# Up projection of a ConvFFN: seven of 22 pairs of channel tiles by seven half products, with sums of weights formed in DRAM

## The chip, the cores and the metric

One core of one Trainium2 chip. Its engines each run an instruction queue of their own: TensorE (PE) multiplies, VectorE (DVE) and ScalarE (ACT) work elementwise, GpSimd (POOL) does a little of both and issues the DMAs that add into their target, SyncE (SP) issues the other DMAs. The metric is the device time of one execution in microseconds (us).

## What is computed

The kernel is one layer of an encoder block, for 512 tokens of 1024 channels in fp32: a layer norm, then a mixing stage (a scan branch and a sparse attention branch, joined and projected by `w_out`), a layer norm, a feed-forward stage with a causal convolution over time, and a last layer norm. The change is in the feed-forward stage, of which the reference says:

```python
def _conv_ffn(h, w_up, conv_w, conv_b, w_down):
    u = _causal_dwconv(h @ w_up, conv_w, conv_b)
    a, v = jnp.split(u, 2, axis=-1)
    return (jax.nn.silu(a) * v) @ w_down

h = _layernorm(DN_ALPHA * h + mix, ln1_g, ln1_b)
f = _conv_ffn(h, ffn_w_up, ffn_conv_w, ffn_conv_b, ffn_w_down)
```

`w_up` is 1024×5632: 2816 channels for a and as many for v. The convolution has three taps.

## The kernel before

**Products.** Each fp32 operand is split into a high and a low half (ACT copies the high one, DVE subtracts for the low one), and a product is three matmuls, hi·hi, lo·hi and hi·lo (`mm3`, whose matmuls stand under L231). A weight block of 128×1024 comes by one SP DMA into one of four `wraw` buffers, then ACT forms `whi` (L188) and DVE `wlo` (L189), in one of three pairs of `whi`/`wlo` buffers (`wload`, L178). The code asks the scheduler to place these steps early.

**w_out.** The projection before the feed-forward stage accumulates in eight PSUM banks, two for each of the four tiles of 128 tokens (L255). Token tile after token tile is finished, normalized (DVE, POOL) and transposed, four blocks of 128 at a time, into one of two `ptr` banks (L1177). ACT and DVE split the transposed block into `h1hi` and `h1lo` (L174, L175), the token operand of the up projection. The low halves of the last of w_out's other operand, `mlo`, lie in the two buffers of the tag `y8`.

**Up projection.** 44 tiles of 128 channels, two by two: tile 2n is a, tile 2n+1 is v, so that pair n gives 128 channels of the result. A tile is 8 blocks of 128 input channels times three matmuls of 512 token columns, 24 matmuls. The first three tiles run in halves of 256 tokens, 144 matmuls, so that they can begin before the last token tiles are transposed. The banks go round among the `pacc` tiles and `pa`, `pb`, `pc`.

**Behind each pair** stands `up_out`: for a and for v one ACT operation (the last tap and the bias, L1270) and two DVE operations (the other taps, L1273) read the tile from PSUM; then Silu on ACT (L1276) and the product on DVE (L1278). Every second pair goes on into `operands` (L1247 to L1253), which forms the sums of channels that the down projection uses. The down projection itself already goes by seven half products, and the sums of its weights are formed in DRAM during the up projection, by `sums_of`: one copy on SP's queue and three adding DMAs on POOL's queue for each of 11 blocks (`sd_d`, L206 to L219).

**Attention.** Earlier, in the attention branch, POOL adds mask and bias of a head and a query block into `tm` (L986), 64 times; DVE and ACT then form the softmax.

Of the kernel before, what the change touches and what calls it, by code (L numbers as in the profile page):

```python
# [9 lines left out]
F32 = mybir.dt.float32  # L10
# [6 lines left out]
P = 128  # L17
# [40 lines left out]
def tok(i):  # L58
    return slice(i * P, (i + 1) * P)
# [11 lines left out]
def block_kernel(ctx, tc, A, out):  # L71
# [16 lines left out]
    def wt(tag, shape, name, dtype=F32):  # L88
        return wk.tile(shape, dtype, name=name, tag=tag, bufs=BUFS[tag])
# [9 lines left out]
    def ct(shape, name, dtype=F32):  # L99
        return cst.tile(shape, dtype, name=name, tag=name)  # L100
# [59 lines left out]
    nc.gpsimd.memset(e_t, math.e)  # L160


    last_pow, last_w = [None], [None]

    def rsqrt_small(src, scale, eps, n, i=0):

# [6 lines left out]
    def split(hi, lo, src):  # L173
        nc.scalar.activation(hi, src, AF.Copy)  # L174
        return nc.vector.tensor_tensor(lo, src, hi.bitcast(F32), OP.subtract)  # L175

    def wload(src, ahead=400, dst=None):

        cols = src.shape[1]
        with tc.high_priority(offset=ahead):  # L180
            raw = wrw.tile([P, D], F32, name="wraw", tag="wraw")
            last_w[0] = nc.sync.dma_start(raw[:, :cols], src)
            if dst is None:
                hi = whl.tile([P, D], F32R, name="whi", tag="whi")
                lo = whl.tile([P, D], F32R, name="wlo", tag="wlo")
            else:
                hi, lo = dst
            nc.scalar.activation(hi[:, :cols], raw[:, :cols], AF.Copy)  # L188
            nc.vector.tensor_tensor(lo[:, :cols], raw[:, :cols], hi[:, :cols].bitcast(F32),  # L189
                                    OP.subtract)  # L190
        return hi, lo

    def w_halves(name, s):
# [9 lines left out]
    def w_(name, s, **kw):  # L203
        return wload(A[name][s], **kw)

    def sums_of(c):  # L206

        S_, B_ = sd_d[c], A["w_dq"][c]

        def copy():  # L210
            with tc.issue_after(last_w[0].ins):
                nc.sync.dma_start(S_, B_)

        def add(dst, src):
            with tc.issue_after(last_pow[0].ins):
                nc.gpsimd.dma_start(dst, src, accum_op=OP.add)  # L216
# [750 lines left out]
    class Head:  # L967
# [12 lines left out]
        def exp(self, i):  # L980
            Q, Kh, Kl = self.qk
            hh = self.hh
            K = P * (i + 1)
            f = max(K - 2 * P, 0)
            tm = wt("tn", [P, 2 * P], "tm")
            nc.gpsimd.tensor_tensor(tm[:, :K - f], maskt[i][:, f:], self.toe[:, 2 * P - K + f:], OP.add)  # L986
            p = tr_tile()
            mm(p[:, :K], Q[:, hh, tok(i)], Kh[:, hh, :K], start=True, stop=False)
            mm(p[:, :K], Q[:, hh, tok(i)], Kl[hh][:, :K], start=False, stop=True)
            if i > 1:  # L990
                self.L.append(wt("v", [P, T], "l"))
            l = self.L[i]
            ic = slice(i, i + 1)
            if f:
                nc.vector.tensor_tensor_reduce(l[:, :f], p[:, :f], maskt[i][:, :f], scale=1.0, scalar=3.0e38,
                                               op0=OP.add, op1=OP.min, accum_out=self.mf[:, ic])
            nc.vector.tensor_tensor_reduce(l[:, f:K], p[:, f:K], tm[:, :K - f], scale=1.0,  # L997
                                           scalar=self.mf[:, ic] if f else 3.0e38,
                                           op0=OP.add, op1=OP.min, accum_out=self.mn[:, ic])
            nc.scalar.activation(l[:, :K], l[:, :K], AF.Exp, bias=self.mn[:, ic], scale=-1.0,  # L1000
                                 accum_out=self.sm[:, ic])
# [157 lines left out]
    for i in range(NT):  # L1159
        for h in range(2):  # L1160
            for k in range(KR, KD):
                tok_mm(accs[2 * i + h], mT[k], wo[k], i, h, False, k == KD - 1)
            ws = half_of(h)
            nc.vector.scalar_tensor_tensor(h1[i][:, ws], h1[i][:, ws], ALPHA, accs[2 * i + h], OP.mult, OP.add)
        mv, rs = ln_stats(h1[i])
        for j in range(2):
            t = h1[i][:, half_of(j)]
            if j == 1 and i < NT - 1:
                nc.vector.tensor_scalar(t, t, mv[:, 0:1], rs, OP.subtract, OP.mult)
                nc.gpsimd.tensor_tensor(t, t, l1r["g", j], OP.mult)  # L1170
                nc.gpsimd.tensor_tensor(t, t, l1r["b", j], OP.add)
            else:
                nc.vector.scalar_tensor_tensor(t, t, mv[:, 0:1], l1r["g", j], OP.subtract, OP.mult)
                nc.vector.scalar_tensor_tensor(t, t, rs, l1r["b", j], OP.mult, OP.add)
            tr = v3(tr_tile())
            for k in range(4):
                nc.tensor.transpose(tr[:, k], h1[i][:, tok(4 * j + k)], ident)  # L1177
# [7 lines left out]
    NS, NC = 8, KF // 2  # L1185
    TH = T // 2
    L_, R_ = slice(0, TH), slice(TH, T)
    fp = E(tc.tile_pool(name="f", bufs=1, reuse_waits="tile"))
    cnt = {"x": 0, "f": 0}
    f8 = {}  # L1190

# [68 lines left out]
    def up_out(n, pa, pb):  # L1260
        uv = []
        key = [(2 * n + j + 1) * UP - 2 * KF * UP if n > KF - 3 else None for j in range(2)]

        def k(j, t):
            return None if key[j] is None else key[j] + t

        for j, p in enumerate((pa, pb)):
            c = n + j * KF
            y = wt("v", [P, T], "u")
            at(S, k(j, 0), nc.scalar.activation(y, p, AF.Identity, bias=fb[:, c:c + 1], scale=fw[:, 88 + c:89 + c]))  # L1270
            for i in (1, 0):
                d = 2 - i
                at(V, k(j, 1.5), nc.vector.scalar_tensor_tensor(  # L1273
                    y[:, d:], p[:, :T - d], fw[:, 44 * i + c:44 * i + c + 1], y[:, d:], OP.mult, OP.add))
            uv.append(y)
        at(S, k(0, 3), nc.scalar.activation(uv[0], uv[0], AF.Silu))  # L1276
        if n < 2 * NS:
            nc.vector.tensor_tensor(uv[0], uv[0], uv[1], OP.mult)  # L1278
            even.append(uv[0])
            if len(even) == 2:  # L1280
                operands(*even)
                even.clear()
        else:
            fO[n] = o_tile()
            tt(k(1, 2.5), fO[n], uv[0], uv[1], OP.mult)

    w = [w_("w_up", s) for s in range(3)]
    accs = [acc_tile() for _ in range(3)]
    for ts in (slice(0, 2 * P), slice(2 * P, T)):
        for j in range(3):  # L1290
            proj(accs[j][:, ts], w[j], [[x[:, ts] for x in h] for h in h1T])
    pend = accs
    done = 0
    jobs = [sums_of(c) for c in range(NC)]
    for s in range(3, 2 * KF + 1):
        if len(pend) >= 2:
            up_out(done, pend[0], pend[1])
            done += 1
            pend = pend[2:]
        if s < 2 * KF:  # L1300
            p = acc_tile() if s % 2 else any_tile("abc")
            proj(p, w_("w_up", s), h1T)
            pend.append(p)
            if s == 36:
                mark = last_w[0]
        if s % 3 == 0:
            for c, j in enumerate(jobs):
                if 0 <= s // 3 - 1 - c < 4:
                    j[s // 3 - 1 - c]()
        if s == 8:  # L1310
            for i in range(NT):
                nc.sync.dma_start(h1_d[:, i], h1[i])

# [329 lines left out]
```

## Time and profile before

| What | Value |
|---|---|
| Median of three runs | 1083.81 us (1083.75 to 1083.89) |
| The profiled execution's own time | 1083.8 us |
| Its span (first to last instruction) | 1082.1 us |
| PE busy | 1070.2 us, 99% |
| DVE busy | 829.6 us, 77% |
| ACT busy | 503.1 us, 46% |
| POOL busy | 195.1 us, 18% |
| w_out ends, up projection begins | 727.28 us |
| First full tile of the up projection begins | 746.68 us |

All positions are microseconds from the span's start. The span is 1.7 us shorter than the execution's own time. A row of a group reads: line, engine, operation, out<-in, shapes and count; busy time and mean ns of one; idle time of the engine just before them, and what ended it. Matmul ends are modelled and overlap the next start, so the time from start to start is what one costs.

### The profile page before, as it was taken

The numbers are of one execution on the slowest core, as the hardware profiler recorded it, in microseconds if no ns is written. First come the engines' busy times: TensorE is split into PE (matmuls) and PEld (weight loads), VectorE is DVE, ScalarE is ACT, GpSimd is POOL, SyncE is SP. The second block draws the span as 40 slices with busy tenths as digits, with TensorE's granted clock in tenths as the row PEclk, the third lists the DMA queues.
The fourth block names the chain that finished last, engine by engine and source line by source line (L and its number), as shares of the span: only waits on it lengthen the run. The fifth ranks groups of instructions, "written<-read, shape, count | busy, mean of one in ns | idle before, by whom it ended". The sixth has DMA issues, their size and how long they took to land.

```text
span 1082.1 us, 14878 instructions
## 1 busy us (share of the span) xinstructions
PE 1070.2 (99%) x5397; PEld 890.4 (82%) x5397; DVE 829.6 (77%) x1509; ACT 503.1 (46%) x876; POOL 195.1 (18%) x214
## 2 busy tenths in 40 slices
PE   8999999999999999999999999999999999999997
PEld 7888888888888888888778778889888888888886
DVE  7667787886999996558989958665766676559697
ACT  5444665563643642355556434313544444345631
POOL 3000203203013023013323442042111111000001
PEclk9999999999999999999999999999999999999999
DMA  7442423474344243322212454818889888226653
GB/s 286 141 146 88 134 80 119 144 217 137 96 119 137 79 141 108 124 86 74 88 56 72 141 195 154 293 59 198 195 237 228 202 237 230 96 90 231 212 181 123
DMA packets 54378, 161.64 MB, mean 149 GB/s; under 512 B 6273, under 2 KB 10929, under 8 KB 54129
## 3 DMA queue, kind: packets, MB, share of 16 engines
q1 hardware_dynamic: 49552, 149.16, 41.9%
q0 software_dynamic: 4752, 11.54, 7.3%
q8 instruction: 42, 0.69, 0.3%
q14 instruction: 32, 0.25, 0.1%
HBM read 152.12 MB, written 34.76 MB: 173 GB/s over the span
## 4 chain that ended last, share of the span: by engine, by line
PE 97%; DMA 1%; DVE 1%; ACT 0%; issue 0%; POOL 0%; DVEq 0%
PE pacc L231 65%; PE pc L231 8%; PE ptr L231 6%; PE pb L231 6%; PE pa L231 5%; PE pacc L255 2%; PE ptr L255 1%; PE pa L234 1%; PE ptr L234 1%; PE pb L234 1%; DMA htok_d<-x 1%; PE pb L255 1%; PE pc L255 1%; PE pa L255 1%; DMA x<-in_x_dram 0%; DVE x_st L339 0%
## 5 line engine op out<-in xcount | busy, mean ns | idle before, releaser
L189 DVE TENSOR_TENSOR wlo<-wraw,whi 128x1024 fp32r<-128x1024 f32 x141 | 184.4, 1308 | 124.3 <-ACT whi L188 123.1
L188 ACT ACTIVATE whi<-wraw 128x1024 fp32r<-128x1024 f32 x141 | 149.1, 1058 | 225.4 <-PE pacc L231 148.7
L231 PE MATMUL pacc<-hhi,whi 128*128 128x512 f32 (+1 forms) x536 | 216.4, 404 | 0.8 <-ACT hhi L398 0.8
L231 PE MATMUL pacc<-hlo,whi 128*128 128x512 f32 (+1 forms) x536 | 209.9, 392 | 0.5 <-DVE hlo L401 0.5
L231 PE MATMUL pacc<-hhi,wlo 128*128 128x512 f32 (+1 forms) x536 | 208.4, 391 | 0.1
L231 PEld LDWEIGHTS pacc<-hlo,whi 128*128 128x128 f32 (+1 forms) x536 | 100.5, 187 | 23.6 <-DVE hlo L401 1.8
L231 PEld LDWEIGHTS pacc<-hhi,whi 128*128 128x128 f32 (+1 forms) x536 | 100.8, 188 | 20.0 <-issue 1.4
L231 PEld LDWEIGHTS pacc<-hhi,wlo 128*128 128x128 f32 (+1 forms) x536 | 100.7, 188 | 18.2 <-DVE wlo L363 0.4
L986 POOL TENSOR_TENSOR tm<-mask,toe 128x128 f32<-128x128 f32 (+1 forms) x64 | 45.0, 706 | 193.0 <-DVE mn L997 117.0
L231 PE MATMUL pacc<-h1hi,wlo 128*128 128x512 f32 (+1 forms) x216 | 79.0, 366 | 0.0
L231 PE MATMUL pacc<-h1hi,whi 128*128 128x512 f32 (+1 forms) x216 | 78.9, 366 | 0.0
L231 PE MATMUL pacc<-h1lo,whi 128*128 128x512 f32 (+1 forms) x216 | 78.7, 366 | 0.0
L621 DVE SCALAR_TENSOR_TENSOR cv<-pacc,cwb,cv 128x511 f32<-128x511 f32 (+2 forms) x72 | 53.2, 740 | 0.3
L231 PE MATMUL pacc<-yhi,whi 128*128 128x512 f32 x128 | 50.3, 395 | 0.0
L231 PE MATMUL pacc<-ylo,whi 128*128 128x512 f32 x128 | 49.9, 390 | 0.0
L231 PE MATMUL pacc<-yhi,wlo 128*128 128x512 f32 x128 | 49.8, 389 | 0.0
L1000 ACT ACTIVATE l<-l,mn 128x128 f32<-128x128 f32 (+1 forms) x64 | 35.7, 558 | 30.3 <-DVE mn L997 28.9
L231 PEld LDWEIGHTS pacc<-h1hi,wlo 128*128 128x128 f32 x216 | 40.8, 189 | 6.7
L231 PEld LDWEIGHTS pacc<-h1hi,whi 128*128 128x128 f32 x216 | 40.7, 188 | 6.5
L231 PEld LDWEIGHTS pacc<-h1lo,whi 128*128 128x128 f32 x216 | 40.6, 189 | 6.5
L783 POOL TENSOR_TENSOR v<-v,eaB 128x384 f32<-128x384 f32 x16 | 17.0, 1077 | 152.5 <-DVE v L782 95.5
L216 POOL DMA_DIRECT2D sd_d<-sd_d x22 | 18.0, 820 | 142.8 <-DMA sd_d<-in_w_dq_dram 77.6
(602 smaller groups left out, 2366.2 us busy)
## 6 DMA issues: line engine op xcount, KB each, us to landing
wraw<-in_w_up_dram SPq DMA_DIRECT2D x44, 512.0 KB, 5.8
wraw<-in_w_xbc_dram SPq DMA_DIRECT2D x24, 512.0 KB, 3.5
G<-ac_d SPq DMA_DIRECT2D x16, 512.0 KB, 5.4
wraw<-in_w_z_dram SPq DMA_DIRECT2D x16, 512.0 KB, 3.5
wraw<-in_w_br_ssd_dram SPq DMA_DIRECT2D x16, 512.0 KB, 3.5
wraw<-in_w_dq_dram SPq DMA_DIRECT2D x27, 256.0 KB, 3.7
sd_d<-in_w_dq_dram POOLq DMA_DIRECT2D x11, 512.0 KB, 8.2
sd_d<-sd_d POOLq DMA_DIRECT2D x22, 256.0 KB, 6.1
```

What stands on the lines that cost most here:

```text
L188: nc.scalar.activation(hi[:, :cols], raw[:, :cols], AF.Copy)
L189: nc.vector.tensor_tensor(lo[:, :cols], raw[:, :cols], hi[:, :cols].bitcast(F32), OP.subtract)
L216: nc.gpsimd.dma_start(dst, src, accum_op=OP.add)
L231: pe(nc.tensor.matmul(p, a, b, start=start, stop=stop).ins)
L234: pe(nc.tensor.transpose(p, a, b).ins)
L255: nc.tensor.matmul(p, x[a][:, tok(i)], w[b][h], start=first and j == 0, stop=last and j == 2)
L621: nc.vector.scalar_tensor_tensor(y[:, d:], p[:, :T - d], cwb[:, 24 * k + c:24 * k + c + 1], y[:, d:], OP.mult, OP.add)
L783: nc.gpsimd.tensor_tensor(v[:, P:], v[:, P:], eaB[:, P:], OP.add)
L986: nc.gpsimd.tensor_tensor(tm[:, :K - f], maskt[i][:, f:], self.toe[:, 2 * P - K + f:], OP.add)
L1000: nc.scalar.activation(l[:, :K], l[:, :K], AF.Exp, bias=self.mn[:, ic], scale=-1.0, accum_out=self.sm[:, ic])
```

## The change

Seven pairs (n = 4, 5, 7, 8, 10, 11, 12) are computed as a 2×2 block product: two channel tiles (a, v), two halves of the input channels, two halves of the tokens. Instead of eight half products there are seven, of sums of blocks. What it does:

- **Sums of weights** (`up_sums`): for each of these pairs four blocks of sums in DRAM (`su_d`), by two copies on SP's queue and three adding DMAs on POOL's. They are issued during attention, one step behind each `tm`.
- **Sums of tokens** (`form_T`): while ACT splits a transposed block into `h1hi`, it also copies it in fp32 into `h32`, which takes the two `y8` buffers; DVE forms four sums in place and ACT and DVE split them into `Thi`/`Tlo`, in a pool that closes after the last of these pairs; the pool `f` opens then.
- **The products** (`seven`): 7×4×3 = 84 matmuls of 256 columns. The weights are 3.5 blocks of 128×1024 in four `wraw` buffers, by six DMAs, in place of two blocks by two DMAs. One ACT copy and five DVE operations combine the products into c1 and c2, in SBUF, in one buffer `uv` of the tags `k4` and `g4`, which held `h1`; the store of `h1` to DRAM is issued at step 3 in place of step 8.
- **`up_out`** reads c1 and c2 where it read PSUM; c2 is the negative of the v tile, so its taps are negated copies (`nfw`). The taps of a and v are also written alternately, for all pairs.

```diff
+SEVEN = (4, 5, 7, 8, 10, 11, 12)
...
+    def add(dst, src):
+        with tc.issue_after(last_pow[0].ins):
+            nc.gpsimd.dma_start(dst, src, accum_op=OP.add)
+    def up_sums(n):
+        S_, a, b = su_d[n], A["w_up"][2 * n], A["w_up"][2 * n + 1]
+        def copy():
+            with tc.issue_after(last_w[0].ins):
+                nc.sync.dma_start(S_[:, 0:2], A["w_up"][2 * n:2 * n + 2, :, :T].rearrange("j p t -> p j t"))
+                nc.sync.dma_start(S_[:, 2:4], a.rearrange("p (j t) -> p j t", j=2))
+        return [copy, lambda: add(S_[:, 0:2], b.rearrange("p (j t) -> p j t", j=2)),
+                lambda: add(S_[:, 2], S_[:, 1]), lambda: add(S_[:, 3], S_[:, 2])]
...
+            last_pow[0] = nc.gpsimd.tensor_tensor(tm[:, :K - f], maskt[i][:, f:], self.toe[:, 2 * P - K + f:], OP.add)
+            if ahead:
+                ahead.pop(0)()
...
+    ahead, ups = [lambda: None] * 2, [up_sums(n) for n in SEVEN]
+    for m in range(len(ups) + 3):
+        for q in range(4):
+            ahead.append(ups[m - q][q] if 0 <= m - q < len(ups) else lambda: None)
+        ahead.append(lambda: None)
...
+    h32 = [wt("y8", [P, 4, T], "h32") for _ in range(2)]
...
             split(h1hi[:, ks, tok(i)], h1lo[:, ks, tok(i)], tr)
+            nc.scalar.activation(h32[j][:, :, tok(i)], tr, AF.Copy)
...
+            taps = [nfw[:, i, n:n + 1] if j and n in SEVEN else fw[:, 44 * i + c:44 * i + c + 1] for i in range(3)]
+            at(S, k(j, 0), nc.scalar.activation(y, p, AF.Identity, bias=fb[:, c:c + 1], scale=taps[2]))
+            uv.append((y, p, taps))
+        for i in (1, 0):
+            d = 2 - i
+            for j, (y, p, taps) in enumerate(uv):
+                at(V, k(j, 1.5), nc.vector.scalar_tensor_tensor(y[:, d:], p[:, :T - d], taps[i], y[:, d:],
+                                                                OP.mult, OP.add))
+        uv = [y for y, *_ in uv]
...
+    nfw = ct([P, 3, KF], "nfw")
+    nc.vector.tensor_scalar(nfw, fw.rearrange("p (i c) -> p i c", i=3)[:, :, KF:], -1.0, None, OP.mult)
+    Thi, Tlo = [tp.tile([P, 4, 4, TH], F32R, name=n, tag=n) for n in ("Thi", "Tlo")]
+    def form_T():
+        b11, b12, b21, b22 = [t[:, :, c] for t in h32 for c in (L_, R_)]
+        nc.vector.tensor_tensor(b11, b11, b12, OP.subtract)
+        nc.vector.tensor_tensor(b12, b22, b12, OP.subtract)
+        yield
+        nc.vector.tensor_tensor(b22, b22, b11, OP.add)
+        nc.vector.tensor_tensor(b21, b22, b21, OP.subtract)
+        yield
+        for j, t in ((1, b22), (2, b12), (0, b11), (3, b21)):
+            split(Thi[:, j], Tlo[:, j], t)
+            if j == 2:
+                yield
+        yield
+    def w_block(*srcs):
+        n = len(srcs) * T if len(srcs[0].shape) == 2 else D
+        with tc.high_priority(offset=400):
+            raw = wrw.tile([P, D], F32, name="wraw", tag="wraw")
+            for j, src in enumerate(srcs):
+                d = raw[:, half_of(j)] if n == len(srcs) * T else raw.rearrange("p (j t) -> p j t", j=2)
+                last_w[0] = nc.sync.dma_start(d, src)
+            hi, lo = [whl.tile([P, D], F32R, name=n_, tag=n_) for n_ in ("whi", "wlo")]
+            split(hi[:, :n], lo[:, :n], raw[:, :n])
+        return [(hi[:, half_of(j)], lo[:, half_of(j)]) for j in range(n // T)]
+    def seven(n):
+        a, b, S_ = A["w_up"][2 * n], A["w_up"][2 * n + 1], su_d[n]
+        Bq = {(k, c): [(h1hi[:, 4 * k + q, s_], h1lo[:, 4 * k + q, s_]) for q in range(4)]
+              for k in range(2) for c, s_ in enumerate((L_, R_))}
+        Tq = [[(Thi[:, j, q], Tlo[:, j, q]) for q in range(4)] for j in range(4)]
+        def product(p, w, r):
+            for k in range(4):
+                mm3(p, w, tok(k), r[k], k == 0, k == 3)
+        uv = wt("k4" if n % 2 else "g4", [P, D], "uv")
+        c1, c2 = uv[:, half_of(0)], uv[:, half_of(1)]
+        u1, u4, u2, u3 = [uv[:, j * TH:(j + 1) * TH] for j in range(4)]
+        tt = nc.vector.tensor_tensor
+        Z, W = tr_tile(), tr_tile()
+        a11, y2 = w_block(a[:, :T], S_[:, 2])
+        y3, y1 = w_block(S_[:, 0:2])
+        product(Z[:, L_], a11, Bq[0, 0])
+        product(Z[:, R_], y2, Tq[1])
+        nc.scalar.activation(u1, Z[:, L_], AF.Copy)
+        tt(u2, u1, Z[:, R_], OP.subtract)
+        a22, a12 = w_block(b[:, T:], a[:, T:])
+        product(W[:, L_], y3, Tq[2])
+        tt(u3, u2, W[:, L_], OP.add)
+        Y = acc_tile()
+        product(Y[:, R_], y1, Tq[0])
+        y4, = w_block(S_[:, 3])
+        product(Y[:, L_], a22, Tq[3])
+        tt(u4, u2, Y[:, R_], OP.add)
+        pair_ = [P, 2, TH]
+        tt(c2.rearrange("p (h t) -> p h t", h=2), u3[:, None, :].to_broadcast(pair_), Y.rearrange("p (h t) -> p h t", h=2),
+           OP.add)
+        X = any_tile("abc")
+        product(X[:, L_], a12, Bq[1, 0])
+        product(X[:, R_], y4, Bq[1, 1])
+        tt(c1, c1, X, OP.add)
+        return [c1, c2]
...
+    T_steps = form_T()
+    next(T_steps)
...
+        if s // 2 == max(SEVEN) + 1 and fp is None:
+            tp_c.__exit__(None, None, None)
+            fp = E(tc.tile_pool(name="f", bufs=1, reuse_waits="tile"))
+        if s // 2 in SEVEN:
+            if s % 2 == 0:
+                pend += seven(s // 2)
+        elif s < 2 * KF:
...
+        if s > 3:
+            with tc.issue_after(last_lo[0].ins):
+                next(T_steps, None)
...
-        if s == 8:
+        if s == 3:
             for i in range(NT):
                 nc.sync.dma_start(h1_d[:, i], h1[i])
```

**PE, end of w_out, before.** `pb` and `pc` are the two banks of the last token tile, `mhi` and `mlo` its operands, `wo` and `wh` the weights, and `ptr` the transposes of token tile 1:

```order
L255 MATMUL pb_6518<-wo20_6580,mhi_6309 128x512
L255 MATMUL pb_6518<-wo20_6580,mlo_6252 128x512
L1177 MATMUL ptr_6751<-ident_102,h1_6221 128x128 x4
L255 MATMUL pb_6518<-wo21_6581,mhi_6309 128x512
L255 MATMUL pb_6518<-wo30_6586,mhi_6347 128x512
L255 MATMUL pb_6518<-wo30_6586,mlo_6252 128x512
L255 MATMUL pb_6518<-wo31_6587,mhi_6347 128x512
L255 MATMUL pb_6518<-wo40_6592,mhi_6385 128x512
L1177 MATMUL ptr_6761<-ident_102,h1_6221 128x128 x4
L255 MATMUL pb_6518<-wo40_6592,mlo_6253 128x512
```

The same transposes on PE in the changed kernel, at the end of `pc`; `pacc` are the first three tiles of the up projection:

```order
L268 MATMUL pc_6557<-wh_6659,mlo_6289 128x512
L268 MATMUL pc_6557<-wh_6661,mhi_6535 128x512
L1199 MATMUL ptr_6791<-ident_102,h1_6257 128x128 x4
L1199 MATMUL ptr_6802<-ident_102,h1_6257 128x128 x4
L244 MATMUL pacc_6971<-h1hi_6543,whi_6955 128x256
L244 MATMUL pacc_6971<-h1hi_6543,wlo_6956 128x256
L244 MATMUL pacc_6972<-h1hi_6543,whi_6961 128x256
L244 MATMUL pacc_6972<-h1hi_6543,wlo_6962 128x256
```

Token tile 1's two groups of transposes stood among the matmuls of `pb` and now stand behind the last matmul of `pc`, directly ahead of the first products of the up projection.

**DVE, up projection, before**, a stretch of three tiles; `wlo` are splits of weight blocks, `u` the taps and the product:

```order
L189 TENSOR_TENSOR wlo<-wraw,whi 128x1024
L1273 SCALAR_TENSOR_TENSOR u<-pacc,pvec,u 128x511
L1273 SCALAR_TENSOR_TENSOR u<-pacc,pvec,u 128x510
L1278 TENSOR_TENSOR u<-u 128x512
L189 TENSOR_TENSOR wlo<-wraw,whi 128x1024
L1273 SCALAR_TENSOR_TENSOR u<-pc,pvec,u 128x511
L1273 SCALAR_TENSOR_TENSOR u<-pc,pvec,u 128x510
L189 TENSOR_TENSOR wlo<-wraw,whi 128x1024
L1273 SCALAR_TENSOR_TENSOR u<-pacc,pvec,u 128x511
L1273 SCALAR_TENSOR_TENSOR u<-pacc,pvec,u 128x510
```

And in the changed kernel, in pair 7 of the seven; `uv` are the combinations of its products:

```order
L176 TENSOR_TENSOR wlo<-wraw,whi 128x1024
L1370 TENSOR_TENSOR uv<-uv,ptr 128x256
L1375 TENSOR_TENSOR uv<-uv,pacc 128x256
L176 TENSOR_TENSOR wlo<-wraw,whi 128x1024
L1377 TENSOR_TENSOR uv<-uv,pacc 128x512
L1382 TENSOR_TENSOR uv<-uv,pa 128x512
L176 TENSOR_TENSOR wlo<-wraw,whi 128x1024
L1301 SCALAR_TENSOR_TENSOR u<-uv,pvec,u 128x511
L1301 SCALAR_TENSOR_TENSOR u<-uv,nfw,u 128x511
L1301 SCALAR_TENSOR_TENSOR u<-uv,pvec,u 128x510
L176 TENSOR_TENSOR wlo<-wraw,whi 128x512
L1367 TENSOR_TENSOR uv<-uv,ptr 128x256
```

The splits of weights and the combinations of a pair stand ahead of its taps, and the taps read `uv`. Apart from the DMAs of the sums and `nfw`, no instruction ahead of w_out's transposes changes its place on any engine, and none behind the up projection does.

More of the change, by code (lines that the diff above doesn't have):

```diff
@@ L160, in block_kernel @@
     nc.gpsimd.memset(e_t, math.e)
-    last_pow, last_w = [None], [None]
+    last_pow, last_w, last_lo = [None], [None], [None]
     def rsqrt_small(src, scale, eps, n, i=0):
@@ L188, in wload @@
             nc.scalar.activation(hi[:, :cols], raw[:, :cols], AF.Copy)
-            nc.vector.tensor_tensor(lo[:, :cols], raw[:, :cols], hi[:, :cols].bitcast(F32),
-                                    OP.subtract)
+            last_lo[0] = nc.vector.tensor_tensor(lo[:, :cols], raw[:, :cols], hi[:, :cols].bitcast(F32),
+                                                 OP.subtract)
         return hi, lo
@@ L212, in copy @@
                 nc.sync.dma_start(S_, B_)
-        def add(dst, src):
-            with tc.issue_after(last_pow[0].ins):
-                nc.gpsimd.dma_start(dst, src, accum_op=OP.add)
         return [copy, lambda: add(S_[:, 0:2], B_[:, 1:3]), lambda: add(S_[:, 2], S_[:, 0]),
@@ L305, in block_kernel @@
     sd_d = dram.tile([KF // 2, P, 4, T], F32, name="sd_d")
+    su_d = dram.tile([KF, P, 4, T], F32, name="su_d")
     ms_c = tc.tile_pool(name="mssd", bufs=1)
@@ L985, in exp @@
             tm = wt("tn", [P, 2 * P], "tm")
-            nc.gpsimd.tensor_tensor(tm[:, :K - f], maskt[i][:, f:], self.toe[:, 2 * P - K + f:], OP.add)
+            last_pow[0] = nc.gpsimd.tensor_tensor(tm[:, :K - f], maskt[i][:, f:], self.toe[:, 2 * P - K + f:], OP.add)
+            if ahead:
+                ahead.pop(0)()
             p = tr_tile()
@@ L1187, in block_kernel @@
     L_, R_ = slice(0, TH), slice(TH, T)
-    fp = E(tc.tile_pool(name="f", bufs=1, reuse_waits="tile"))
+    tp_c = tc.tile_pool(name="T", bufs=1, reuse_waits="tile")
+    tp = tp_c.__enter__()
+    fp = None
     cnt = {"x": 0, "f": 0}
@@ L1269, in up_out @@
             y = wt("v", [P, T], "u")
[L1270 to L1275, printed above, removed]
+            taps = [nfw[:, i, n:n + 1] if j and n in SEVEN else fw[:, 44 * i + c:44 * i + c + 1] for i in range(3)]
[7 more added lines that the diff above has]
+        uv = [y for y, *_ in uv]
         at(S, k(0, 3), nc.scalar.activation(uv[0], uv[0], AF.Silu))
@@ L1299, in block_kernel @@
             pend = pend[2:]
-        if s < 2 * KF:
+        if s // 2 == max(SEVEN) + 1 and fp is None:
[5 more added lines that the diff above has]
+        elif s < 2 * KF:
             p = acc_tile() if s % 2 else any_tile("abc")
```

## The prediction

> **What bounds the kernel now.** I read the page first: engine totals, granted clock, chain.
>
> ```profile
> span 1082.1 us, 14878 instructions
> PE 1070.2 (99%) x5397; PEld 890.4 (82%) x5397; DVE 829.6 (77%) x1509; ACT 503.1 (46%) x876; POOL 195.1 (18%) x214
> PEclk9999999999999999999999999999999999999999
> PE 97%; DMA 1%; DVE 1%; ACT 0%; issue 0%; POOL 0%; DVEq 0%
> ```
>
> PE (TensorE) is busy 99% of the span at the full granted clock, and the chain that ended last is 97% PE. So the kernel gets faster where PE has less to do, as long as no other engine becomes late. The second question is who is nearest to being late, and DVE is, at 77%. The profiled run took 1083.8 us, its span 1082.1 and 1.7 outside; the median of the runs is 1083.81, so sums made on the span carry over.
>
> Next the chain in order of time through the up projection (start, us, engine, tile, line, count).
>
> ```profile
> 729.15 6.12 PE pacc L231 x51
> 736.37 10.08 PE pacc L231 x84
> 746.68 5.46 PE pacc L231 x24
> 752.14 5.21 PE pb L231 x23
> 757.36 5.44 PE pacc L231 x24
> ...
> 964.08 5.44 PE pacc L231 x24
> ```
>
> A full tile is 24 matmuls of 512 columns in 5.44 us, 0.2267 each; a matmul of 256 columns takes 0.120 (51 in 6.12, 84 in 10.08). Tile follows tile without a gap, so the up projection is limited by PE alone.
>
> **The products.** A pair of tiles is 48 matmuls of 512 columns today, 2×5.44 = 10.88 us. With seven half products it is 7×4×3 = 84 matmuls of 256 columns, and just such a row stands in the chain: 84 in 10.08 us. A pair saves 0.80, not the eighth of 10.88 (1.36) that counting columns suggests, because a half-width matmul costs more than half. Seven pairs: **−5.6 us**.
>
> By the Trainium skill, "TensorE: Matmul & The Clock Gate", section "Back-to-back issue gap", an isolated matmul of N columns takes N/2.4 + 2.5 ns on a warm clock: 109 and 216 ns, hence 9.17 against 10.36 us a pair and −8.3 in all; the trace disagrees with both figures (120 and 226.7 ns), and the trace decides.
>
> Weight loads could bind narrow matmuls:
>
> ```profile
> L231 PEld LDWEIGHTS pacc<-h1hi,whi 128*128 128x128 f32 x216 | 40.7, 188 | 6.5
> ```
>
> At 0.188 each one after the other, 84 would need 15.8 us; since 84 did fit into 10.08, loads overlap, and nothing is added.
>
> **From w_out into the up projection.** The new h32 copies go into the y8 buffers that hold mlo, read by the last matmuls of w_out. ACT's copy of token tile 0 so waits for these, keeps both ptr banks until then, and the transposes of token tile 1 move behind w_out's last matmul (the order shows it). PE, then ACT and DVE there:
>
> ```profile
> 718.61 0.60 PE L1177 MATMUL ptr<-ident,h 128*128 128x128 f32 x4
> 718.96 0.71 PE L255 MATMUL pb<-wo,mhi 128*128 128x512 f32 x2
> 726.83 0.39 PE L255 MATMUL pc<-wh,mlo 128*128 128x512 f32 x1
> 727.28 0.28 PE L231 MATMUL pacc<-h1hi,whi 128*128 128x256 f32 x1
> 728.55 0.60 PE L1177 MATMUL ptr<-ident,h 128*128 128x128 f32 x4
> 729.19 0.60 ACT L174 ACTIVATE h1hi<-ptr 128x512 fp32r<-128x512 f32 x1 [0.44 <-PE ptr L1177]
> 741.57 1.06 ACT L188 ACTIVATE whi<-wraw 128x1024 fp32r<-128x1024 f32 x1 [4.56 <-PE pacc L231]
> ```
>
> Two transpose blocks at 0.35 (718.61 to 718.96) leave w_out, so it ends 0.71 earlier, at 726.57 in place of 727.28. The last mlo is read until then, so the copy ends near 727.2 (0.60, as for h1hi), h1hi of tile 1 near 727.8 (0.60 again), and the first up matmul starts near 727.9, 0.6 later than now, with the moved blocks in that gap. The rows of h1lo and the next transposes add waits of a few tenths, which the 0.7 of PE work that left the section pays back in part: +0.6. At its end ACT has two late copies (0.60 each) and two splits of T (1.06 each, as the row at 741.57) ahead of the split of the next weight tile; that tile's low half comes some 0.5 late for the first full tile. Together **+1.1**, between 0.5 (less than the gap) and 2.7 (the gap and both splits of T in full).
>
> **DVE in the stage.** Groups of DVE between 740 and 970, then windows (length, then PE, PEld, DVE, ACT, POOL busy; clock; DMA share; GB/s):
>
> ```profile
> L189 DVE TENSOR_TENSOR wlo<-wraw,whi 128x1024 fp32r<-128x1024 f32 x41 | 50.2, 1225 | 71.5 <-ACT whi L188 70.7
> L1273 DVE SCALAR_TENSOR_TENSOR u<-pacc,pvec,u 128x510 f32<-128x510 f32 x23 | 17.2, 749 | 0.7
> L1278 DVE TENSOR_TENSOR u<-u 128x512 f32<-128x512 f32 x16 | 11.1, 692 | 0.6
> L1247 DVE TENSOR_TENSOR s<-u 128x256 f32<-128x256 f32 x8 | 3.4, 424 | 0.3
> 744.40:866.85 122.45, 122.45 (x550) 101.73 (x549) 85.82 (x123) 57.38 (x82) 17.40 (x21) 1.00 0.88 221
> 866.18:877.06 10.88, 10.88 (x49) 9.01 (x49) 8.07 (x12) 5.02 (x7) 1.07 (x2) 1.00 0.85 278
> 877.06:887.94 10.88, 10.88 (x49) 9.01 (x49) 6.83 (x10) 4.81 (x7) 2.25 (x3) 1.00 0.95 217
> ```
>
> A seven pair splits 3.5 weight blocks instead of 2 (three at 1.225 and half of one at 0.69, less two: +1.92) and combines products (three of 256 columns at 0.42, two of 512 at 0.69: +2.64). That is 4.56 a pair, 31.9 for seven. Forming T takes four sums of 1024 columns and four splits; two of the sums are ahead of this stretch, six at 1.225 are in it: 7.4. In all 39.3 of durations. The two last windows hold 21 instructions (12 and 10, one on the border): four at 1.225, eight taps at 0.747, four at 0.69, five at 0.42, 15.74 us, against 8.07 + 6.83 = 14.90 busy. Neighbours overlap by a factor 0.947, so 37.2 come on top of 85.8 in a stretch of 122.45: DVE is full there.
>
> Whether PE waits depends on what DVE does first. The scheduler puts the weight splits ahead, and the conv taps may trail, as a seven pair's sums lie in SBUF. By the order, 154 DVE instructions stand from the split of tile 3 (ended near 744.4) to the first split of pair 12: 34 at 1.225, 42 taps at 0.747, 36 at 0.69, 42 at 0.42, 115.5 us; by 0.947 it is 109.4, ready at 853.8 plus 0.6 of idle. Pair 12 starts at 747.4 (746.3+1.1) + 9×5.44 + 6×10.08 = 856.8: 2.4 us of spare. Without overlap it is 859.9, 3.1 late; the split of tile 26, 168 instructions and 126.2 us, is 2.9 early or 3.7 late against 866.9. I take the overlap, since it was measured, and **+1.0** for single blocks that come late between pairs in succession (0 to 3.7).
>
> **DMA in the stage.** Queue shares, then issues (count, KB, us to landing) between 835 and 880, and SP's wait between 760 and 870:
>
> ```profile
> q1 hardware_dynamic: 1282, 7.07, 45.4%
> q0 software_dynamic: 1068, 2.48, 38.2%
> wraw<-in_w_up_dram SPq DMA_DIRECT2D x9, 512.0 KB, 6.6
> sd_d<-in_w_dq_dram SPq DMA_DIRECT2D x3, 9.5
> SPq L182 <- DVE wlo L189: 100.6, 21, 5.3
> ```
>
> Each seven pair loads 1.5 blocks more (0.79 MB), 5.5 MB in 7×10.08 + 4×5.44 = 92 us. SP today waits for a free buffer nearly all the time (100.6 of 110), so loads run far ahead; what this lead is worth decides two rivals. In the likeliest case the term is nothing.
>
> **Attention.** The sums are formed there, 21 adds on POOL's queue and 14 copies on SP's, behind the tm operations.
>
> ```profile
> 504.00:640.00 136.00, 135.95 (x727) 107.35 (x725) 120.34 (x336) 73.14 (x172) 48.66 (x65) 1.00 0.33 108
> L986 POOL TENSOR_TENSOR tm<-mask,toe 128x256 f32<-128x256 f32 x48 | 36.7, 767 | 99.8 <-DVE mask L606 54.4 <-DVE mn L997 44.7
> L216 POOL DMA_DIRECT2D sd_d<-sd_d x22 | 18.0, 820 | 142.8 <-DMA sd_d<-in_w_dq_dram 77.6 <-DMA sd_d<-sd_d 65.1
> ```
>
> DMA is busy 0.33 there and POOL 48.7 of 136. An add occupies POOL for 0.82 to 1.1 us, but also blocks it until the DMA before it has landed (most of the 142.8). The adds of a pair stand five slots apart, some 10 to 12 us, against landings of 6 to 9.5, and POOL runs up to four tm buffers ahead: nothing, up to 1.0 if some landing is late. The other edits (nfw at the start, one more ACT copy of 0.42 a pair, where ACT has 57.4 of 122 busy, and the four stores of h1_d, which pass five weight loads on SP's queue) I cost at nothing, since neither ACT nor SP is what PE waits for; without their cover the ACT copies would be 2.9, and the stores, 2 MB at the rate below, 6.1 once.
>
> **Sum.** 1083.8 − 5.6 + 1.1 + 1.0 = **1080.3 us**.
>
> **Rivals.** *B: a full DVE or DMA takes most of it back.* Without overlap, DVE is 3.7 late: 1083.8 − 5.6 + 1.1 + 3.7 = 1083.0. DMA gives nearly the same: 7.07 MB in 45.4% of 45 us is 346 GB/s, so 5.5 MB are 15.9 us of all 16 engines, of which 0.12×92 = 11 are free: 4.9 late, 1084.2. The Trainium skill, "DMA: Bandwidth & Descriptors", section "Issuing engines are not separate DMA queues", says that transfers of SP, ACT and POOL interleave on the same 16 engines; the trace agrees in that a 512 KB weight load takes 6.6 us beside the sums. For B: a share of 0.88, and 16 engines at 221 GB/s. Against: 278 GB/s went through at 0.85, and the sums for the down projection may come later. Range 1081.6 to 1086.0.
>
> *C, slower: landing.* Four wraw buffers, and a seven pair uses all four once. Each is taken for landing + 1.06 (ACT) + 1.23 (DVE), which must be within 10.08: a landing above 7.8 us lengthens every seven pair by the excess. At 6.6 there is 1.2 to spare; at 9.5, which the larger copies take beside the same traffic, it is 7×1.7 = 11.9: 1079.3 + 11.9 = 1091.2. From 8.75 on the kernel is slower by over 0.2%. For it: more bytes on engines that are busy 0.88. Against: the nine loads' own 6.6, and pairs 6 and 9 let the loads catch up.
>
> *D, better:* a 256-column matmul at half of 0.2267 would make a pair 9.52 and the gain 9.5, 1076.4 with the same waits. Against: 0.120 in 144 matmuls. *E:* weight loads bind (15.8 a pair): 1083.8 + 7×4.9 = 1118. *F:* the half products don't stream as in that row, say at each change of bank, and gain nothing: 1085.9.
>
> **How the numbers follow.** Forecast (1078.3 to 1081.6) 0.50; B 0.28; C 0.14; D 0.05; E and F 0.03. The range 1078.3 to 1086.0 takes in the forecast and B, leaves out C, D, E, and two in ten at most. About 0.2%, 2.2 us, is what a measurement of this kernel can tell from no change: faster (below 1081.6) is the forecast and D, 0.55; same is B and F, 0.29; slower is C and E, 0.16.
>
> **What would show it.** In the changed trace: seven runs of 84 matmuls in about 10.08 with PE's idle before them under 0.2 each; the first up matmul near 727.9, and the first full tile near 747.4; DVE above 115 of 122 us busy between 745 and 867; w_up landings near 7. Wrong would be: PE idle at the seven pairs released by wlo with DVE busy throughout (B), or by whi with ACT waiting for the DMA and landings beyond 7.8 (C); an attention stage that is longer than before; a matmul spacing other than 0.120.

## The result and the profile after

The changed kernel takes **1091.0 us** (four runs, 1090.32 to 1092.02) against 1083.83 of the kernel before (1083.75 to 1083.89): a ratio of 1.0067, 95% interval 1.0052 to 1.0082. It is 7.2 us slower, where 3.5 less was forecast.

The page of the profile after, its span, its engines and the shares of the chain:

```profile
span 1089.4 us, 15628 instructions
PE 1074.4 (99%) x5649; PEld 898.9 (83%) x5649; DVE 864.8 (79%) x1567; ACT 525.9 (48%) x909; POOL 211.1 (19%) x235
PE 91%; DVE 5%; issue 2%; DMA 1%; ACT 1%; POOL 0%; DVEq 0%; SPq 0%; ACTq 0%; POOLq 0%
```

PE is as busy as before, 99%, and yet its work ends later: such a share says that PE was occupied, not that it was fast. Its chain through the up projection:

```profile
755.57 5.67 PE pb L244 x24
761.24 5.44 PE pacc L244 x24
...
783.00 4.31 PE ptr L244 x36
787.32 2.88 PE pacc L244 x24
790.20 2.88 PE pa L244 x24
793.08 3.00 PE ptr L244 x25
...
808.96 5.25 PE pacc L244 x23
816.98 9.89 DMA wraw<-in_w_up_dram
...
974.52 1.40 PE ptr L244 x6
```

The first product of full width starts at 755.57 (746.45 before, one matmul ahead of the row at 746.68), so 9.1 us are lost ahead of it. The first pair by seven products, 36 + 24 + 24 matmuls, takes 793.08 - 783.00 = 10.08 us, as forecast. At 816.98 the chain runs through a weight load that took 9.89 us to land. Six matmuls of the down projection take 1.40; before, the row was:

```profile
969.52 1.36 PE ptr L231 x6
```

So the loss is not where the change is. Since PE's instructions ahead of w_out's last transposes and behind the up projection stand in the same order in all these kernels, the same matmul can be looked up in each trace. How much later it starts than before, in us, at five positions (of before) and at the end:

| Kernel | 475, ahead of attention | 645, behind it | 690, into w_out | 722 | 985, down projection | end of span |
|---|---|---|---|---|---|---|
| after | +2.85 | +6.38 | +7.70 | +7.38 | +5.32 | +7.3 |
| e5 | -0.12 | +3.39 | +3.39 | +2.44 | -1.28 | -1.3 |
| e7 | -0.09 | -0.06 | -0.06 | -1.01 | -4.74 | -4.3 |
| e10 | -0.03 | +0.01 | +0.01 | -0.94 | -3.47 | -3.0 |
| e11 | +0.07 | +0.27 | +0.27 | +0.27 | -2.75 | -3.1 |
| e12 | -0.04 | +0.04 | +1.43 | +1.44 | +11.41 | +11.6 |

The row "after" shows three losses. 2.85 us are gone by 475, and 2.35 of them by 450, before the first copy of the sums is issued (454.5); all that the change runs until then is nfw's one instruction (0.2 us, at 10.6). Attention loses 3.5 more. Between 645 and the down projection the gain of the up projection is smaller than it should be, and the down projection, which isn't touched, loses 2 again. The other rows are from the experiments.

### The profile page after: what moved, and what is told of

Read it like the earlier page. It is cut to its first block, busy times and chain, and to the rows that moved or that the text cites. A ratio compares the mean times of both kernels' runs of the same rounds, so it can differ in the third digit from the quotient of the medians.

```text
span 1089.4 us, 15628 instructions
## 1 busy us (share of the span) xinstructions
PE 1074.4 (99%) x5649; PEld 898.9 (83%) x5649; DVE 864.8 (79%) x1567; ACT 525.9 (48%) x909; POOL 211.1 (19%) x235
## 4 chain that ended last, share of the span: by engine, by line
PE 91%; DVE 5%; issue 2%; DMA 1%; ACT 1%; POOL 0%; DVEq 0%; SPq 0%; ACTq 0%; POOLq 0%
PE pacc L244 60%; PE ptr L244 8%; PE pc L244 8%; PE pb L244 5%; PE pa L244 4%; PE pacc L268 2%; PE ptr L268 1%; DMA wraw<-in_w_up_dram 1%; PE ptr L247 1%; DVE wlo L190 1%; PE pa L247 1%; DVE l L1013 1%; PE pb L247 1%; PE pc L268 1%; PE pa L268 1%
## 5 line engine op out<-in xcount | busy, mean ns | idle before, releaser
L189 ACT ACTIVATE whi<-wraw 128x1024 fp32r<-128x1024 f32 x127 | 134.3, 1058 | 209.7 <-PE pacc L244 148.4
L190 DVE TENSOR_TENSOR wlo<-wraw,whi 128x1024 fp32r<-128x1024 f32 x127 | 167.2, 1317 | 81.8 <-ACT whi L189 81.3
L1000 POOL TENSOR_TENSOR tm<-mask,toe 128x128 f32<-128x128 f32 (+1 forms) x64 | 47.4, 743 | 188.7 <-DVE mn L1013 112.0
L244 PE MATMUL pacc<-h1hi,wlo 128*128 128x512 f32 (+1 forms) x160 | 57.2, 358 | 0.0
L244 PE MATMUL pacc<-h1hi,whi 128*128 128x512 f32 (+1 forms) x160 | 57.1, 358 | 0.0
L244 PE MATMUL pacc<-h1lo,whi 128*128 128x512 f32 (+1 forms) x160 | 56.8, 359 | 0.0
L175 ACT ACTIVATE whi<-wraw 128x1024 fp32r<-128x1024 f32 (+1 forms) x28 | 26.7, 952 | 37.3 <-PE pacc L244 17.3
L746 ACT ACTIVATE G<-G,acT 128x128 f32<-128x128 f32 x128 | 40.1, 392 | 0.0
L171 POOL TENSOR_TENSOR rs_y<-rs_v,mhalf 128x4 f32<-128x4 f32 (+1 forms) x10 | 10.4, 1043 | 140.8 <-DVE rs_v L169 140.8
```

The lines of the kernel that those rows point to most:

```text
L190: last_lo[0] = nc.vector.tensor_tensor(lo[:, :cols], raw[:, :cols], hi[:, :cols].bitcast(F32), OP.subtract)
L244: pe(nc.tensor.matmul(p, a, b, start=start, stop=stop).ins)
L746: i = nc.scalar.activation(G[:, h, c], G[:, h, c], AF.Relu, bias=acT[:, c, q:q + 1], scale=-1.0)
L1000: last_pow[0] = nc.gpsimd.tensor_tensor(tm[:, :K - f], maskt[i][:, f:], self.toe[:, 2 * P - K + f:], OP.add)
```

## The experiments

The theory after a look at the trace was in two parts: *addresses* (nfw takes 264 bytes of each partition, all buffers behind it move, and matmuls whose operands lie otherwise against each other are spaced wider), and *POOL's adds* (in attention they keep DVE waiting). The rival was *traffic*: the DMAs of the sums slow everything.

**e1: nfw in 320 bytes.**

```diff
-    nfw = ct([P, 3, KF], "nfw")
+    nfw = ct([P, 80], "nfw")[:, :3 * KF].rearrange("p (i c) -> p i c", i=3)
```

> The changed kernel with the constant nfw in a row of 320 bytes instead of 288, so that every buffer allocated behind it begins at a multiple of 64 bytes again, as before; the instructions and their order stay the same. Theory (matmuls whose two operands begin 32 bytes apart modulo 64 are spaced 233 ns instead of 226.7): the first 480 us lose 2.9 less, the two projections ahead of the up projection 1.1 less, the down projection 2.3 less; 1091.0 - 6.3 = about 1085. Rival (the traffic of the sums slows PE): no change, 1091.

Measured: 1089.4 us (1088.72 to 1090.97; before 1083.57 beside it). The theory in this form is wrong: a multiple of 64 bytes is not what counts. But something moved. Windows of 40 us in the down projection of the kernel before, of the changed one, and of e1 (length; then PE, PEld, DVE, ACT and POOL with their instructions; then the granted clock, the busy share of the DMA engines and their GB/s):

```profile
990.00:1030.00 40.00, 40.00 (x178) 33.11 (x177) 31.32 (x49) 25.57 (x42) 0.00 (x0) 1.00 0.62 199
```

```profile
990.00:1030.00 40.00, 40.00 (x174) 32.41 (x173) 32.34 (x52) 24.99 (x42) 0.00 (x0) 1.00 0.65 206
```

```profile
990.00:1030.00 40.00, 40.00 (x177) 32.90 (x176) 33.41 (x55) 25.14 (x42) 0.00 (x0) 1.00 0.65 213
```

PE is busy for all 40 us at the full clock in each, but gets through 178, 174 and 177 matmuls. Worked out from the starts of 512-column matmuls between 975 and 1030, the mean spacing is 226.8 ns before, 232.2 after, 228.5 in e1.

**e2: the kernel before, moved by 32 bytes.**

```diff
+    ct([P, 8], "shift")
     w = [w_("w_up", s) for s in range(3)]
```

> The kernel before with nothing changed but a constant of 32 bytes that is never used, which moves the buffers behind it by 32 bytes. Theory: spacing 233 ns in the down projection and in the projections ahead of the up projection, 226.7 in the up projection itself (both operands move there); about +6 us, 1090. Rival (traffic of the sums): 1083.8, since there are none here.

Measured: 1090.55 us (1090.46 to 1090.7), ratio 1.0063 (1.0051 to 1.0076), with not one instruction changed. In the down projection it is as slow as the changed kernel, 232.2 ns; in the up projection, where both operands move together, the spacing is 226.7 as before:

```profile
990.00:1030.00 40.00, 40.00 (x174) 32.36 (x173) 32.33 (x51) 24.56 (x42) 0.00 (x0) 1.00 0.62 203
```

Traffic as the cause of the spacing is out: here there is none beyond what the kernel before has.

**e5: nfw in the unused 288 bytes at the far end.** The kernel allocates each partition from two ends, so there are near buffers (low addresses) and far ones; nfw is a near one, and a pool `pad` of 288 bytes that nothing uses lies at the far end. With nfw in it, every buffer has its old address, and the program is the changed kernel's.

```diff
-    pad.tile([P, PAD], F32, name="pad")
+    room_ = pad.tile([P, PAD], F32, name="pad")
...
-    nfw = ct([P, 3, KF], "nfw")
+    nfw = room_[:, :3 * KF].rearrange("p (i c) -> p i c", i=3)
```

> The changed kernel with nfw placed in the 288 bytes that lay unused at the far end, so that every buffer has the address that it had before; instructions and their order stay the same. A row of 320 bytes (e1) took back only part, so the theory is now: what counts is how far the two operands of a matmul lie apart, modulo something larger than 64 bytes (before: a multiple of 1024), and all of the 226.7 ns come back. Then the 2.9 us of the first 480, the 1.1 ahead of the up projection and the 2.3 of the down projection go: 1091.0 - 6.3 = 1084.7, with attention 3.5 longer than before as it was. Rival (the spacing comes from something else in the changed kernel, its traffic or its code): 1089 as e1.

Measured: 1083.71 us (1082.57 to 1085.52), ratio to before 1.0001 (0.9992 to 1.0009): 7.3 us below the changed kernel, by addresses alone. In the table its first column is back at zero, and from 690 on it gains 4.7. (Its profiled run is one of its quicker ones, with a span 1.3 us below before's, while its median is level with before.) The chain of e5, and 119.5 us of the up projection, from 0.6 ahead of its first full tile to 0.9 ahead of the end of pair 12:

```profile
777.90 4.31 PE ptr L244 x36
...
787.98 3.00 PE ptr L244 x25
...
968.24 1.36 PE ptr L244 x6
```

```profile
749.90:869.40 119.50, 119.50 (x804) 110.79 (x803) 111.07 (x166) 70.53 (x100) 14.09 (x17) 1.00 0.88 247
```

A pair takes 10.08, six matmuls of the down projection 1.36 again, PE has no idle time in the stretch, and DVE is busy 111.1 of 119.5.

**e9 and e13: the kernel before, moved by 128 and by 256 bytes** (the edit of e2 with 32 and 64 words).

> The kernel before with an unused constant of 128 bytes (e2 had 32): the near buffers move by 128 against the far ones. Shifts of 32 and of 288 gave the same slow pattern, 320 another. Theory A (the distance counts modulo 128): no change, 1083.7, spacing 226.7 in the down projection. Theory B (modulo 256): a third pattern, spacing between 227.5 and 235 somewhere, 1085 to 1090.

> The kernel before with an unused constant of 256 bytes. Shifts of 32 and 288 bytes gave the same spacing in every stage, which speaks for a period of 256. Theory (the distance of a matmul's operands counts modulo 256): no change, 1083.7, spacing 226.7 in the down projection. Rival (modulo 512 or more): slow like the other shifts, 1088 to 1091.

Measured: 1089.97 us (1089.9 to 1090.01) for 128 bytes, spacing 231.3 ns; 1083.76 (1083.5 to 1084.21) for 256, ratio 0.9999 (0.9990 to 1.0009), spacing 226.8:

```profile
990.00:1030.00 40.00, 40.00 (x175) 32.62 (x174) 32.07 (x51) 24.22 (x41) 0.00 (x0) 1.00 0.62 200
```

```profile
990.00:1030.00 40.00, 40.00 (x179) 33.10 (x178) 31.34 (x49) 25.62 (x42) 0.00 (x0) 1.00 0.64 200
```

A period of 256 bytes fits all six shifts (0, 32, 128, 256, 288 and 320). Before, the weights `whi` began at byte 25,280 and the far buffers such as `yhi` at 155,328, 508×256 apart; the changed kernel moved `whi` to 25,568. Where both operands are near ones, as `h1hi` and `whi` in the up projection, they move together, and the full tile stayed at 5.44 us in the changed kernel; so it is the distance that counts, not the address of one operand.

**e3: no adds in attention** (with e1's row of 320 bytes).

```diff
-        return [copy, lambda: add(...), lambda: add(...), lambda: add(...)]
+        return [copy] + [lambda: None] * 3
```

> As e1_pad64, with the 21 adding DMAs left out of attention (the 14 copies stay; su_d then holds no sums, so that part of the computation is missing). Theory (POOL's adds, and the tm operations that they push back, keep DVE's longer operations waiting in attention, 3.5 us): 3.5 below e1_pad64, about 1081.3. Rival (the DMA traffic of copies and loads does it, or the weight loads): within 1 us of e1_pad64.

Measured: 1085.03 us (1084.38 to 1088.69), 4.4 below e1; from 475 to 645, by the same matmuls as in the table, its trace loses 0.1 us where e1 loses 3.7. The 1081.3 was missed since e1 itself lay 4.4 higher than was expected of it. What is still open is whether POOL's work in an add or its traffic does it.

**e8: plain copies instead of adds** (from e5; the same blocks on SP's queue).

```diff
-        return [copy, lambda: add(S_[:, 0:2], b...), lambda: add(S_[:, 2], S_[:, 1]), ...]
+        return [copy, lambda: plain(S_[:, 0:2], b...), lambda: plain(S_[:, 2], S_[:, 1]), ...]
```

> As e5_nfw_in_pad, with the 21 adding DMAs of attention replaced by as many plain copies of the same blocks on SP's queue (su_d then holds no sums, so that part of the computation is missing). Theory (POOL's part in an add holds up DVE's longer operations): attention as before the change, 3.5 below e5_nfw_in_pad, about 1081.2. Rival (the adds' traffic in DRAM holds up attention): as e5_nfw_in_pad within 1 us.

Measured: 1080.54 us (1079.85 to 1081.09), 3.2 below e5: with nearly the same bytes (152 GB/s from 490 to 640 against 161 in e5, though the DMA engines are busy 0.48 of it against 0.69), and none of POOL's work, attention is as before. The groups of DVE that differ in attention (480 to 640), in before, e5 and e8:

```profile
L189 DVE TENSOR_TENSOR wlo<-wraw,whi 128x1024 fp32r<-128x1024 f32 x20 | 28.6, 1432 | 0.3 <-ACT whi L188 0.2
L946 DVE CAST Kh<-Kh 64x512 fp32r<-64x512 f32 x12 | 6.1, 506 | 0.3
```

```profile
L190 DVE TENSOR_TENSOR wlo<-wraw,whi 128x1024 fp32r<-128x1024 f32 x20 | 30.4, 1522 | 1.1 <-ACT whi L189 1.0
L960 DVE CAST Kh<-Kh 64x512 fp32r<-64x512 f32 x12 | 8.0, 664 | 0.3
```

```profile
L190 DVE TENSOR_TENSOR wlo<-wraw,whi 128x1024 fp32r<-128x1024 f32 x20 | 27.9, 1393 | 0.4 <-ACT whi L189 0.2
L964 DVE CAST Kh<-Kh 64x512 fp32r<-64x512 f32 x12 | 6.1, 504 | 0.3
```

With the adds the same 20 splits and 12 casts take 1.8 + 1.9 = 3.7 us longer, beside the 3.5 of the table. Nearly all of it lies in five instructions: three splits of 2.35 us, which take 1.65 at the same place before, and two casts of 1.54 in place of 0.71. PE's waits in the changed kernel from 470 to 740 are all for DVE, 2.3 us, and before and e8 have none:

```profile
PE pb L247 <- DVE l L1027: 1.4, 4, 0.8
PE pc L244 <- DVE pt L1032: 0.9, 2, 0.5
```

One of the long splits in the changed kernel, DVE and then POOL (start, us):

```profile
516.95 2.35 DVE L190 TENSOR_TENSOR wlo<-wraw,whi 128x1024 fp32r<-128x1024 f32 x1
```

```profile
513.53 0.74 POOL L1000 TENSOR_TENSOR tm<-mask,toe 128x256 f32<-128x256 f32 x1 [0.23 <-DVE mn L1013]
514.22 0.96 POOL L209 DMA_DIRECT2D su_d<-su_d  x1
...
516.64 0.80 POOL L209 DMA_DIRECT2D su_d<-su_d  x1
517.21 1.00 POOL L1000 TENSOR_TENSOR tm<-mask,toe 128x256 f32<-128x256 f32 x1
```

A split that takes 1.22 us alone takes 2.35 while POOL works at an add and then at a `tm`, which without the add would have stood ahead by half a microsecond (the `tm` before it ended at 516.69). The Trainium skill, "SBUF — State Buffer", section "Who interferes with whom", has the rule: a DVE instruction with two inputs in SBUF contends with a GpSimd instruction that reads SBUF, a cast in a two-port mode with any, and the later one blocks wholly. The trace agrees (1.13 us longer, under a `tm` of 1.00).

**e4: the sums formed ahead of attention** (with e1's 320 bytes): all seven pairs of copies and all 21 adds earlier.

```diff
+    copies += [u[0] for u in ups]
     run([in_x(3, 3), in_z(3, 0), in_z(3, 1), in_z(3, 2), out_br(2, 0)],
...
+    for q in (1, 2, 3):
+        for u in ups:
+            u[q]()
     qkv, nxt = [], []
```

> As e1_pad64, with the sums of weights formed earlier: the copies among the weight loads of the last two scan groups, the 21 adds in three rounds on POOL's queue right ahead of attention, where DVE is busy about half the time. Theory: attention as before the change, 3.5 below e1_pad64, about 1081.3, if the traffic doesn't delay the weight loads there. Rival: the traffic delays them, or the adds hold POOL beyond the first tm; then 1083 or more.

Measured: 1086.28 us (1085.07 to 1089.6), 3.1 below e1, but within the rival's range. From 475 to 645 e4 still loses 1.0 us. The adds ended at 487.8, the first `tm` of a new head came behind them, and DVE's operation that reads it began at 488.37, 2.5 us later than in e1:

```profile
488.37 0.29 DVE L1020 CUSTOM_DVE_ANT_0 l<-ptr,tm 128x128 f32<-128x128 f32 x1 [3.07 <-POOL tm L1007]
```

**e6 and e10: both causes taken away.** e5 with the copies and the first seven adds already among the scan's work, the other 14 adds ahead of attention; e10 is the same kernel again, and the trace is e10's.

```diff
+        if g == 2:
+            early += [u[0] for u in ups]
...
+    early += [u[1] for u in ups]
     run([in_x(3, 3), in_z(3, 0), in_z(3, 1), in_z(3, 2), out_br(2, 0)],
...
+    for q in (2, 3):
+        for u in ups:
+            u[q]()
     qkv, nxt = [], []
```

> As e5_nfw_in_pad, with the sums of weights formed earlier: copies from the last part of the third scan group on, the seven adds of 512 KB among the scan's POOL work, the 14 of 256 KB in a row ahead of attention. Theory: no add is left in attention, its 3.5 us go; 1084.7 - 3.5 = 1081.2, if POOL is through before the first tm and the landings in the up projection (up to 12.8 us in e1) cost 1 to 2 as so far. Rival (the traffic only moves, and the weight loads there come late): 1083 or more.

> The kernel of e6_pad_early2 once more, for an undisturbed trace: 1080.4 within 0.5; attention within 0.3 us of before; in the up projection one or two waits of 0.5 to 2 us behind weight loads that land after more than 8 us.

Measured: 1080.36 us, ratio 0.9972 (0.9962 to 0.9981), and 1080.89 (1079.88 to 1081.78), ratio 0.9973 (0.9962 to 0.9983). This version is faster than both kernels, by 3 us than the one before. In e10's trace attention costs nothing, and one wait of 1.2 us behind a late weight load remains in the up projection.

**e7: e6 without the adds for the down projection.**

> As e6_pad_early2, with the 33 adding DMAs left out that form the sums of the down projection's weights during the up projection (their 11 copies stay; the output then lacks these sums). Theory (what is left of waiting in the up projection are weight loads that land late among that traffic): w_up and su_d loads land in under 7 us, no wait over 0.3 us ahead of a product, 1 to 2 us below e6_pad_early2, about 1079.7 (1083.8 - 5.6 + 1.4 of the start of the up projection). Rival (DVE is the bound there): as e6_pad_early2 within 0.5.

Measured: 1078.93 us (1078.74 to 1079.91), 1.4 below e6 and 2.0 below e10. DMA issues between 760 and 880, of the changed kernel and of e7:

```profile
wraw<-in_w_up_dram SPq DMA_DIRECT2D x10, 512.0 KB, 8.6
wraw<-su_d SPq DMA_DIRECT2D x6, 512.0 KB, 6.0
```

```profile
wraw<-in_w_up_dram SPq DMA_DIRECT2D x12, 512.0 KB, 5.1
wraw<-su_d SPq DMA_DIRECT2D x6, 512.0 KB, 3.8
```

In the changed kernel 17 of 49 loads there take over 7.8 us, up to 12.2; in e10 it is 13 of 49, in e7 none, and there PE has no wait. POOL's adds do not slow DVE here: its splits take 1.22 us in e7 as in e10. So what still costs something in this stage is the landing.

**e11: h32 by POOL.**

```diff
-            nc.scalar.activation(h32[j][:, :, tok(i)], tr, AF.Copy)
+    for c in range(2):
+        for j in range(2):
+            ...
+                last_pow[0] = nc.gpsimd.tensor_tensor(h32[j][:, :, x_[2]], h1hi[x_]..., h1lo[x_]..., OP.add)
```

> As e6_pad_early2, with h32 formed by POOL from the halves (high plus low, four additions of 128x1024 behind the last layer norm's work) instead of by ACT copies from PSUM, so that nothing holds the ptr banks until w_out has ended; the token sums start one tile later. Theory (the changed start of the up projection costs 1.4 us, since transposes of token tile 1 wait behind w_out): the transposes stand where they were before the change, the first full tile starts 1.0 to 1.4 earlier against w_out's end, 1079.2. Rival (POOL's additions, at 2.8 us each, hold up DVE or end after the token sums need them): 1080.4 or more.

Measured: 1081.12 us (1080.68 to 1082.77), 0.8 above e6 and 0.2 above e10: no gain, as the rival has it. DVE, then POOL, then PE's wait in e11:

```profile
729.98 0.74 DVE L1205 SCALAR_TENSOR_TENSOR h<-h,ln_mv,l1g 128x512 f32<-128x512 f32 x1
...
731.24 2.81 DVE L1205 SCALAR_TENSOR_TENSOR h<-h,ln_mv,l1g 128x512 f32<-128x512 f32 x1
```

```profile
731.10 5.19 POOL L1216 TENSOR_TENSOR h<-h1hi,h1lo 128x1024 f32<-128x1024 f32 x2
```

```profile
PE ptr L1209 <- issue: 1.4, 1, 1.4
```

The same DVE instruction takes 0.74 us, and 2.81 when POOL's addition began just ahead of it. The last token tile comes late, and PE waits 1.4 us for its transposes: what e11 gains in w_out's last tile it gives back here.

**e12: nine pairs in a row.**

```diff
-SEVEN = (4, 5, 7, 8, 10, 11, 12)
+SEVEN = (4, 5, 6, 7, 8, 9, 10, 11, 12)
```

> As e11_h32_pool, with pairs 6 and 9 by seven products too (nine in a row), and the last adds of each pair's sums behind the last layer norm input's POOL work rather than ahead of attention. Theory (PE's gain is 0.80 a pair, and DVE and the landings carry seven of nine with little to spare): two pairs more give -1.6, but DVE needs 9.1 us more in a stretch that is full, and no pair of two loads stands between: waits of 3 us or more, 1080.5 or more. Rival (DVE has spare room, since taps may trail): 1.6 below e11_h32_pool.

Measured: 1092.39 us (1090.89 to 1095.42), 11.3 above e11. Part of it, 1.4, is lost by 690, where the last adds were put. The largest of PE's waits in e12, one of ACT's, and its loads between 770 and 890:

```profile
PE ptr L244 <- DVE wlo L176: 2.7, 2, 1.7
PE pb L244 <- ACT whi L175: 2.3, 2, 1.4
PE ptr L244 <- ACT whi L175: 2.3, 2, 1.4
PE pb L244 <- ACT whi L189: 2.1, 1, 2.1
```

```profile
ACT whi L175 <- DMA wraw<-su_d: 16.7, 7, 4.0
```

```profile
wraw<-in_w_up_dram SPq DMA_DIRECT2D x7, 512.0 KB, 9.9
```

These waits end with ACT's `whi` more often than with DVE, and ACT waits for the loads. Probably they don't catch up without a pair of two loads between; since e12 also moved adds, that is not shown by itself. That both get late is shown; how much each would cost alone was not tried.

## Why the prediction was wrong

**What held.** The 10.08 us of a pair, hence -5.6. With the address effect gone (e5, e7) the table gives -4.7 from 690 to 985 with no wait, so the start of the up projection costs 0.9 where the prediction had 1.1. Waits in the stage, from start to start of PE's matmuls: 0 (e5, in the profiled run), 1.2 (e10) and 1.2 (the changed kernel, at 827), around the 1.0 taken. That this term fits is luck, since it was set down for DVE, and the waits that came are behind late loads. DVE did not become the bound: the working gave 123.0 us of DVE in 122.45, and it was busy 111 of 119.5 in e5, as the taps trailed behind the stretch. Rival C's mechanism, landings over 7.8 us, is there, but it stopped PE once in the changed kernel and not in every pair; that its 1091.2 lies beside the 1091.0 is chance. The sum of what was looked at comes out: 1083.8 - 5.6 + 1.1 + 1.0 = 1080.3, and e6, which has only these terms, measures 1080.4 (1080.9 as e10).

**What failed: "The other edits (nfw at the start, ...) I cost at nothing".** nfw's one DVE instruction costs nothing indeed. Its 264 bytes moved all near buffers behind it by 288, and with them 2.9 us were lost by 475, 2.0 more up to 722 (after +7.38 less +6.38, against e5's +2.44 less +3.39), and 2.0 from 985 to the end, where after goes from +5.32 to +7.3 and e5 stays at -1.3. That is 6.9. Between 722 and 985 the two differ by 1.7 more: 1.2 are the changed kernel's wait at 827, of which e5's profiled run has none, and the rest is again addresses, 0.3 of it in the down projection ahead of 985, where e2 loses as much. So addresses cost 7.3, as the medians of the changed kernel and e5 say; e5's other runs, up to 3.0 us longer than its quickest, have no trace. The prediction asked of each edit what runs, and never where things lie.

**What failed: the attention term, "nothing, up to 1.0 if some landing is late".** It is 3.5 (3.4 between the medians of e5 and e6). The prediction priced an add by POOL's free time and by its landing, and POOL did have that time; but it did not ask which DVE instructions POOL's work keeps from running, in the one stage where DVE is busy 120.3 of 136 us and PE has no slack against it: with the adds PE waits 2.3 us for DVE there. A longer attention stage stood among the prediction's own signs of being wrong. The rows of before had it: the same split took 1.432 us in the mean there and 1.225 in the up projection.

So the kernel is slower for neither of the reasons that the rivals named: 1080.3 + 7.3 + 3.4 = 1091.0. The last two terms are differences of medians down to e6, so what this sum tests is the 1080.3.

## What to carry to other kernels

A new constant is an edit to every buffer behind it: compare the addresses of two builds, and keep the distance of a matmul's two operands a multiple of 256 bytes, as it was here before the change. Work for POOL goes where DVE has time to spare, since a DMA issue there can push an operation under a long one of DVE. A busy share of 99% hides a slower instruction: compare how many instructions a window of the same work holds.

## What the runs showed of the hardware

PE's rate depends on where its operands lie: shifts of 32, 128, 288 and 320 bytes between near and far buffers space 512-column matmuls by 228.5 to 232.2 ns in the down projection, shifts of 0 and 256 by 226.7 to 226.8. That is 0.8 to 2.4% of a matmul, and 6 to 7 us of this kernel. The Trainium skill, "SBUF — State Buffer", section "Who interferes with whom", says that PE never waits for another engine, and gives it separate ports for the moving operand and for weight loads; the runs don't contradict that, as e2 slows PE without an instruction more on any other engine, but which of the two accesses is held up they don't show.
